# Two FFN norm rows by way of DRAM, and another order at the end of a convolution module, in a decoder trunk on one core

## The chip, the cores and the metric

The kernel runs on one core of one Trainium2 chip. The metric is the device time of one launch in microseconds. The engines are named as in the profile: PE is the matrix engine (PEld its weight loads), DVE the vector engine, ACT the scalar engine, POOL the GpSimd engine, SP the queue that issues most DMAs.

## The reference, cut to what matters

A trunk of four pre-norm residual sub-layers over 512 tokens and 1024 channels, in fp32: a retention and pooling mixer, an FFN, a convolution module, and a second FFN, with a final norm.

```python
def rms_norm(x, g):
    y = x * lax.rsqrt(jnp.mean(x * x, axis=-1, keepdims=True) + EPS)
    return y * g

def swiglu(h, w_gate, w_up, w_down):
    return (jax.nn.silu(h @ w_gate) * (h @ w_up)) @ w_down

def conformer_conv(h, w_pw1, b_pw1, w_dw, b_dw, ln_g, ln_b, w_pw2, b_pw2):
    a, gate = jnp.split(h @ w_pw1 + b_pw1, 2, axis=-1)
    u = a * jax.nn.sigmoid(gate)
    dw = causal_depthwise_conv(u, w_dw, width=31) + b_dw
    mu = jnp.mean(dw, axis=-1, keepdims=True)
    var = jnp.mean(jnp.square(dw - mu), axis=-1, keepdims=True)
    z = jax.nn.silu((dw - mu) * lax.rsqrt(var + EPS) * ln_g + ln_b)
    return z @ w_pw2 + b_pw2

x = x + swiglu(rms_norm(x, ffn_g), ...)      # after the mixer and after the conv module
x = x + conformer_conv(rms_norm(x, mix_g), ...)
```

## The kernel before

The activation X lies in SBUF with channels on partitions (eight tiles of 128) and the 512 tokens along the free side; the halves of 256 tokens are called A and B. Products run in fp32r, with each operand split into a high part and a rest: `mm3` issues high x high, high x rest and rest x high (lines 199 to 201). Splits are made while the kernel runs, ACT casting the high part and DVE or POOL's accumulating DMA making the rest; raw weight chunks of 1 MB arrive by SP's queue in two buffers (`wr`).

**Norm rows.** A norm needs one factor for each token, along the free side and equal on all partitions. `token_sums` multiplies `acc` (the squares summed over the channel tiles, 128 x 512) with a column of ones: four fp32 matmuls with 128 of the tokens each as weights, so that the sums come out with token 128t + p on partition p, column t of `ps_ms`. `inv_rms` makes the inverse root of them on DVE (`rs_y`, 128 x 4, three Newton steps, lines 264 to 271). `spread` turns it into a row on all partitions: four fp32 matmuls of `rs_y`'s broadcast columns with the unit matrix into `ps_rms` (line 289), and a copy by ACT into `bc_rms` (line 293). fp32 matmuls are two records each in the trace. In an FFN the factor is not applied to the input but to gate and up after their products (`hidden`, line 884, DVE). gu0 and gu1 are the first two column blocks of gate and up; `spread` stands between the products k = 4 and k = 5 of gu1, and `token_sums` at gu1's start.

**The conv module** is written in the order in which each engine is to run it. `proj(j)` is the first pointwise product of channel tile j (value and gate), `gated(j)` its sigmoid gate: DVE scales both by the norm's row, ACT takes the sigmoid (line 1192), DVE multiplies into `u` (line 1196). The channels' convolution runs in two ways. Tiles 0 to 2 are done on DVE, 31 taps each (`some_taps(n)`, line 1329, one multiply-add of 128 x 512 per tap). Tiles 3 to 7 are done on PE (`conv_tile`, line 1229): `to_rows` writes four shifted copies of `u` by DMA (tile `R`; for tile 5 the tile named `zh`, still unused then), and eight groups of four 32 x 32 diagonal products per quadrant add up the taps. `pivot_sum` and `pivot_mean` form a pivot from two tiles (token sums again, PE line 281, behind DVE's line 1301), which is spread as `mus` and taken from every tile before sums and squares are added up (`into_sums` for DVE's tiles, `pivot_tile` for PE's). `stats` makes mean and inverse deviation of a half (`ps_ms`, `ps_mu`, `ps_lrs`). `centre`, `swish`, `z_hi`, `z_lo` then make z, two tiles at a time, and split it (high `zh` by ACT, line 1288; rest `zl` by DVE). `out_proj(w, j, cols)` multiplies tiles j and j + 1 of z with four column blocks of the second pointwise weights into the PSUM pairs q0 and q1, for half A and then for half B; for each pair, `high_first` issues the eight products of the high part before the four with z's rest. `split_rest` splits a raw weight chunk in two parts with ACT and POOL's DMA (lines 1351, 1352); written as a generator, it is begun ahead of a `gated` and finished within it. PSUM holds three pairs of banks (`pmm`) and two single banks (`paux`).

Of the kernel before, what the change touches and what calls it, by code (L numbers as in the profile page):

```python
# [10 lines left out]
F32 = mybir.dt.float32  # L11
# [3 lines left out]
ALU = mybir.AluOpType  # L15
# [68 lines left out]
def trunk(ctx: ExitStack, tc: tile.TileContext, a: dict):  # L84
# [10 lines left out]
    paux = ctx.enter_context(tc.tile_pool(name="paux", bufs=2, space=PSUM))  # L95

# [115 lines left out]
    def high_first(ps, wh, wl, xh, xl, cols, ks, k0=0):  # L212

        for low in range(2):
            for k in ks:
                for i in range(2):
                    c = slice(i * P, (i + 1) * P)
                    o = ps[:, i, cols]
                    if low:
                        nc.tensor.matmul(o, lhsT=wh[:, k - k0, c], rhs=xl[k][:, cols], start=False, stop=k == KT - 1)  # L220
                    else:
                        nc.tensor.matmul(o, lhsT=wh[:, k - k0, c], rhs=xh[k][:, cols], start=k == 0, stop=False)
                        nc.tensor.matmul(o, lhsT=wl[:, k - k0, c], rhs=xh[k][:, cols], start=False, stop=False)

# [50 lines left out]
    def token_sums(acc, cols=FULL):  # L275

        ps = paux.tile([P, S], F32, tag="aux", name="ps_ms")
        n = (cols.stop - cols.start) // P
        for t in range(n):
            at = cols.start + t * P  # L280
            nc.tensor.matmul(ps[:, t:t + 1], lhsT=acc[:, at:at + P], rhs=ones, start=True, stop=True)
# [14 lines left out]
    def inv_rms(acc):  # L296
        v = sm.tile([P, NT], F32, tag="ms", name="ms")
        nc.vector.tensor_scalar(v, token_sums(acc), 0.5 / D, 0.5 * EPS, ALU.mult, ALU.add)
# [398 lines left out]
    def ffn_in(layer, acc, gain, fx, fl, fh, fe, ff):  # L697
# [278 lines left out]
        r = inv_rms(acc)  # L976
# [10 lines left out]
        feature_major(ps[1], *w, xgh, xgl, between={5: lambda: row.update(rb=spread(r, "rms"))})  # L987
# [178 lines left out]
    def conv(acc):  # L1166
        with ExitStack() as m:
# [54 lines left out]
            def conv_tile(j, cols, between={}, ps=None):  # L1222
                ps = ps if ps is not None else paux.tile([P, S], F32, tag="aux", name=f"ps_c{j}")
                n = cols.stop - cols.start
                for g in range(8):
# [137 lines left out]
            def out_proj(w, j, cols):  # L1363

                for i, q in enumerate((q0, q1)):
                    c = slice(2 * P * i, 2 * P * (i + 1))
                    high_first(q, w[0][:, :, c], w[1][:, :, c], zhs, zls, cols, range(j, j + 2), j // 4 * 4)
# [4 lines left out]
            with tc.manual_schedule(engines={mybir.EngineType.PE, mybir.EngineType.DVE, mybir.EngineType.Activation,  # L1372
# [43 lines left out]
                rest = split_rest()  # L1416
                next(rest)
                c3 = conv_tile(3, FULL)
                some_taps(1)
                gated(5, pss[5], FULL, two_taps, rest)  # L1420
                start_load()
                to_rows(5, FULL)
                bias_tile(3, c3)
                some_taps(14)
# [181 lines left out]
```

## Time and the profile before

| | us |
|---|---|
| median of 3 runs | 1047.19 (1046.95 to 1047.38) |
| the profiled execution | 1047.62 |
| its span, first to last instruction | 1045.8 |
| PE busy | 1035.9 (99%) |
| DVE busy | 850.5 (81%) |
| ACT busy | 515.9 (49%) |
| mean granted TensorE clock | 0.998 |

Rows of the profile read: start (or busy time), duration, engine, line, operation, output<-inputs, shape, and in brackets the idle time ahead of it with what ended it. xN joins N like instructions. A matmul's end is modelled and overlaps the next one's start, so PE is read by differences of starts. In lists of waits the numbers are the total in us, the count, and the longest. In lists of DMA issues the last number is the median time in us from issue to landing.

### The profile page before, as it was taken

Reading aid. Unit: us, or ns where it says so; the run is one execution under the profiler, and the core shown is the slowest. Engines: PE = TensorE matmul, PEld = TensorE weight load, DVE = VectorE, ACT = ScalarE, POOL = GpSimd, SP = SyncE. Lnnn points to the kernel's source line nnn. Section 1 sums busy time; section 2 is a strip of 40 time slices with the busy share of each in tenths; the row PEclk is TensorE's granted clock in tenths of the full one; section 3 lists DMA queues with packets and bytes.
Section 4 is the critical chain, followed back from the end, with each engine's and each line's share of the span. In section 5 each row is a group of like instructions: output and inputs, shape, how many; then the busy total and the mean of one; then the engine's idle time right before and its main releaser. Section 6 shows DMA issues by size and latency. Waiting matters only on the chain.

```text
span 1045.8 us, 16517 instructions
## 1 busy us (share of the span) xinstructions
PE 1035.9 (99%) x6705; PEld 907.9 (87%) x6705; DVE 850.5 (81%) x1297; ACT 515.9 (49%) x881; POOL 32.5 (3%) x33
## 2 busy tenths in 40 slices
PE   9999999999999999999999999999999999999997
PEld 7878888899999999998888665988999999999987
DVE  7888735889988889997779797859999888899855
ACT  8543134765454545543444325656654455445434
POOL 0000000100000000001121100000000000000000
PEclk9999999999999999999999999999999999999999
DMA  8322122643323322333248996146233332323122
GB/s 300 132 81 81 41 81 88 184 136 116 111 92 104 119 91 92 122 118 125 81 94 188 222 189 149 59 139 174 72 121 121 102 121 76 112 96 122 41 81 81
DMA packets 38108, 121.63 MB, mean 116 GB/s; under 512 B 4112, under 2 KB 13328, under 8 KB 29584
## 3 DMA queue, kind: packets, MB, share of 16 engines
q1 hardware_dynamic: 34432, 107.99, 32.4%
q0 software_dynamic: 3456, 12.58, 6.3%
q8 instruction: 52, 0.85, 0.3%
q14 instruction: 24, 0.20, 0.1%
q10 hardware_dynamic: 144, 0.00, 0.0%
HBM read 100.36 MB, written 2.10 MB: 98 GB/s over the span
## 4 chain that ended last, share of the span: by engine, by line
PE 88%; DVE 6%; ACT 2%; DMA 2%; issue 1%; DVEq 0%; ACTq 0%
PE ps_x L854 19%; PE ps_y L854 10%; PE ps_dn L199 7%; PE ps_dn L200 7%; PE ps_dn L201 7%; PE ps_z L854 5%; PE ps_c L1229 2%; PE ps_gu L201 2%; PE ps_gu L199 2%; PE ps_gu L200 2%; PE ps_pw L199 2%; PE ps_pw L201 2%; PE ps_pw L200 2%; DMA wr<-in_w_pw 2%; PE ps_wo L201 1%; PE ps_wo L200 1%
## 5 line engine op out<-in xcount | busy, mean ns | idle before, releaser
L854 PE MATMUL ps_x<-th,w 128*128 128x256 f32 x608 | 115.9, 276 | 0.3 <-ACT sn L929 0.3
L765 DVE TENSOR_TENSOR wg<-wg 128x512 f32<-128x512 f32 x152 | 105.3, 693 | 5.1
L774 ACT CAST w<-wg 128x512 fp32r<-128x512 f32 x152 | 82.9, 618 | 37.3 <-PE ps_y L854 36.0
L854 PEld LDWEIGHTS ps_x<-th,w 128*128 128x128 f32 x608 | 97.2, 188 | 0.5 <-ACT sn L929 0.5
L779 DVE TENSOR_TENSOR w<-wg,w 128x2048 fp32r<-128x2048 f32 x38 | 87.1, 2291 | 10.5 <-ACT w L774 10.1
L854 PE MATMUL ps_x<-tl,w 128*128 128x256 f32 x304 | 83.9, 276 | 0.0
L311 DVE TENSOR_TENSOR X<-X,ps_dn 128x1024 f32<-128x1024 f32 x46 | 56.0, 1218 | 18.6 <-PE ps_dn L201 18.6
L183 ACT CAST w<-wr 128x2048 fp32r<-128x2048 f32 (+2 forms) x22 | 34.8, 1599 | 56.6 <-PE ps_g L573 21.8
L199 PE MATMUL ps_dn<-hh,dh0d 128*128 128x512 f32 x152 | 59.4, 391 | 0.0
L200 PE MATMUL ps_dn<-hl,dh0d 128*128 128x512 f32 x152 | 59.4, 391 | 0.0
L201 PE MATMUL ps_dn<-hh,dl0d 128*128 128x512 f32 x152 | 59.2, 390 | 0.1
L854 PE MATMUL ps_y<-th,w 128*128 128x256 f32 x304 | 57.9, 276 | 0.0
L854 PE MATMUL ps_y<-xgh,w 128*128 128x256 f32 x304 | 57.9, 276 | 0.0
L854 PEld LDWEIGHTS ps_x<-tl,w 128*128 128x128 f32 x304 | 57.1, 188 | 0.0
L939 ACT COPY sn<-ps_x 128x256 f32<-128x256 f32 x38 | 14.2, 374 | 85.9 <-PE ps_x L854 85.9
L200 PE MATMUL ps_dn<-hl,dh1d 128*128 128x512 f32 x144 | 56.2, 391 | 0.0
L199 PE MATMUL ps_dn<-hh,dh1d 128*128 128x512 f32 x144 | 56.2, 391 | 0.0
L201 PE MATMUL ps_dn<-hh,dl1d 128*128 128x512 f32 x144 | 56.0, 389 | 0.0
L854 PE MATMUL ps_x<-xgh,w 128*128 128x256 f32 x288 | 55.2, 277 | 0.0
L878 DVE TENSOR_TENSOR hl<-act,hh 128x512 fp32r<-128x512 f32 x44 | 30.5, 692 | 26.3 <-ACT hh L877 26.1
L877 ACT CAST hh<-act 128x512 fp32r<-128x512 f32 x44 | 27.3, 621 | 48.0 <-DVE act L872 44.0
L199 PE MATMUL ps_pw<-xgh,w 128*128 128x512 f32 x128 | 50.3, 393 | 0.0
(346 smaller groups left out, 3098.9 us busy)
## 6 DMA issues: line engine op xcount, KB each, us to landing
wg<-in_w_gu SPq DMA_DIRECT2D x38, 1024.0 KB, 4.9
dr<-in_w_dn SPq DMA_DIRECT2D x64, 256.0 KB, 2.9
w<-wr POOLq DMA_DIRECT2D x24, 512.0 KB, 5.3
wr<-in_w_pw SPq DMA_DIRECT2D x10, 1024.0 KB, 5.1
wr<-in_w_gu SPq DMA_DIRECT2D x6, 1024.0 KB, 4.9
dr<-in_w_dn SPq DMA_DIRECT2D x32, 192.0 KB, 2.5
wr<-in_w_o SPq DMA_DIRECT2D x4, 1024.0 KB, 4.9
R<-u SPq DMA_DIRECT2D x12, 270.0 KB, 14.6
```

Of the source, the lines that this page charges most:

```text
L183: nc.scalar.copy(wh[:, s], raw[:, s])
L199: nc.tensor.matmul(out, lhsT=wh, rhs=xh, start=start, stop=False)
L200: nc.tensor.matmul(out, lhsT=wh, rhs=xl, start=False, stop=False)
L201: nc.tensor.matmul(out, lhsT=wl, rhs=xh, start=False, stop=stop)
L311: nc.vector.tensor_tensor(xx, xx, ps, sign)
L765: nc.vector.tensor_tensor(o, o, i, ALU.add)
L774: nc.scalar.copy(block(sums[f][0], *SUMS[i]), block(raw_g[f], *SUMS[i]))
L779: nc.vector.tensor_tensor(l, raw_g[f], h.bitcast(F32), ALU.subtract)
L854: nc.tensor.matmul(out, lhsT=u[:, k, :], rhs=v, start=first and k == 0 and n == 0, stop=k == 3 and n == 2, skip_group_check=True)
L877: nc.scalar.copy(hh[f], s)
L878: return lambda: nc.vector.tensor_tensor(hl[f], s, hh[f].bitcast(F32), ALU.subtract)
L1229: nc.tensor.matmul(ps[32 * i:32 * i + 32, :n], lhsT=dgs[j][:, i, g, :], rhs=Rs[j][:, i, 4 * g + cols.start:4 * g + cols.stop], start=g == ...
```

## The change

In both FFNs the norm's row goes by way of DRAM. `token_sums` gets `by=NT` (4): the weights of matmul t are tokens t, t + 4, t + 8 and so on (every fourth fp32 of `acc`), so that partition p holds tokens 4p to 4p + 3. `spread_row` writes `rs_y` to a row in DRAM with one DMA and reads it back with another, broadcast to all 128 partitions; both are issued by SP. `spread` and the ACT copy are gone there; the mixer's and the conv module's norms keep them.

At the end of the conv module:
- tiles 5, 6 and 7 are all done in halves, on PSUM pairs; tile 5's half B is cut in two by tile 7's half A;
- the last gate, gated(7), is done in halves, and it stands ahead of the sums of tiles 1, 4 and 5;
- two splits of weights (`split_rest`) stand behind the gates of tiles 5 and 6 instead of around them, and six more taps ahead of the pivot, two more in tile 4's stage, none at the end;
- the statistics of half A stand at the start of tile 6's half B, the spread of its inverse deviation ahead of tile 7's half B; the mean of half B is spread within an `out_proj`;
- `out_proj` issues all 16 products of z's high part for four column blocks, and then the eight of z's rest;
- in half B tiles 0 and 1 are multiplied, swished and cast one by one.

```diff
+    dr = ctx.enter_context(tc.tile_pool(name="dr", bufs=2, space=bass.MemoryType.DRAM))
...
-    def token_sums(acc, cols=FULL):
+    def token_sums(acc, cols=FULL, by=1):
 
         ps = paux.tile([P, S], F32, tag="aux", name="ps_ms")
         n = (cols.stop - cols.start) // P
+        if by > 1:
+            for t in range(n):
+                nc.tensor.matmul(ps[:, t:t + 1], lhsT=acc.rearrange("p (q t) -> p t q", t=n)[:, t, :], rhs=ones,
+                                 start=True, stop=True)
+            return ps[:, :n]
...
+    def spread_row(v, name):
+
+        row = dr.tile([S], F32, tag="row", name=f"row_{name}")
+        out = wk.tile([P, S], F32, tag=f"bc_{name}", name=f"bc_{name}", bufs=1)
+        nc.sync.dma_start(row.rearrange("(p t) -> p t", t=NT), v)
+        nc.sync.dma_start(out, row.partition_broadcast(P))
+        return out
+
+    def inv_rms(acc, by=1):
         v = sm.tile([P, NT], F32, tag="ms", name="ms")
-        nc.vector.tensor_scalar(v, token_sums(acc), 0.5 / D, 0.5 * EPS, ALU.mult, ALU.add)
+        nc.vector.tensor_scalar(v, token_sums(acc, by=by), 0.5 / D, 0.5 * EPS, ALU.mult, ALU.add)
         return rsqrt(v, NT, "a4")
...
-        r = inv_rms(acc)
+        row["rb"] = spread_row(inv_rms(acc, by=NT), "rms")
         load_gu(f0)
         plain_hi(f0)
...
-        feature_major(ps[1], *w, xgh, xgl, between={5: lambda: row.update(rb=spread(r, "rms"))})
+        feature_major(ps[1], *w, xgh, xgl)
...
-            def conv_tile(j, cols, between={}, ps=None):
+            def conv_tile(j, cols, between={}, ps=None, groups=range(8)):
...
-            def out_proj(w, j, cols):
-
-                for i, q in enumerate((q0, q1)):
-                    c = slice(2 * P * i, 2 * P * (i + 1))
-                    high_first(q, w[0][:, :, c], w[1][:, :, c], zhs, zls, cols, range(j, j + 2), j // 4 * 4)
+            def out_proj(w, j, cols, between=lambda: None):
+
+                (wh, wl), k0 = w, j // 4 * 4
+                for low in range(2):
+                    for i in range(4):
+                        if low == 0 and i == 2:
+                            between()
+                        o, c = (q0, q1)[i // 2][:, i % 2, cols], slice(i * P, (i + 1) * P)
+                        for k in (j, j + 1):
+                            if low:
+                                nc.tensor.matmul(o, lhsT=wh[:, k - k0, c], rhs=zls[k][:, cols], start=False,
+                                                 stop=k == KT - 1)
+                            else:
+                                nc.tensor.matmul(o, lhsT=wh[:, k - k0, c], rhs=zhs[k][:, cols], start=k == 0,
+                                                 stop=False)
+                                nc.tensor.matmul(o, lhsT=wl[:, k - k0, c], rhs=zhs[k][:, cols], start=False,
+                                                 stop=False)
...
                 some_taps(9)
-                rest = split_rest()
-                next(rest)
                 c3 = conv_tile(3, FULL)
                 some_taps(1)
-                gated(5, pss[5], FULL, two_taps, rest)
+                gated(5, pss[5], FULL, two_taps)
                 start_load()
                 to_rows(5, FULL)
+                for _ in split_rest():
+                    pass
                 bias_tile(3, c3)
-                some_taps(14)
+                some_taps(20)
                 proj(6)
-                rest = split_rest()
-                next(rest)
                 pivot_sum()
                 some_taps(1)
                 pivot_mean()
-                gated(6, pss[6], FULL, two_taps, rest)
+                gated(6, pss[6], FULL, two_taps)
                 to_rows(6, FULL)
-                c4 = conv_tile(4, FULL, {5: lambda: spread(row["piv"], "mu", piv)})
-                some_taps(4)
+                for _ in split_rest():
+                    pass
+                c4 = conv_tile(4, FULL, {4: lambda: spread(row["piv"], "mu", piv)})
+                some_taps(6)
                 nc.vector.scalar_tensor_tensor(s1, piv, -2.0, dsum, ALU.mult, ALU.add)
                 for i in PV:
                     into_sums(i, two_taps)
                 proj(7)
-                some_taps(8)
-                into_sums(2)
-                c5 = conv_tile(5, FULL)
-                gated(7, pss[7], FULL)
-                to_rows(7, A)
-                start_load()
-                to_rows(7, B)
+                into_sums(2, two_taps)
+                some_taps(NDVE * CW)
+                p5 = pair("ps_c5")
+                c5 = conv_tile(5, A, ps=p5[:, 0, :])
+                for cols in HALVES:
+                    gated(7, pss[7], cols)
+                    to_rows(7, cols)
+                    if cols is A:
+                        start_load()
                 nc.scalar.activation(warm, warm, AF.Silu)
-                some_taps(NDVE * CW)
-                into_sums(1)
-                pivot_tile(4, c4, FULL)
                 p6, p7 = [pair(f"ps_c{j}") for j in (6, 7)]
                 c6 = conv_tile(6, A, ps=p6[:, 0, :])
-                pivot_tile(5, c5, FULL)
+                pivot_tile(5, c5, A)
+                pivot_tile(4, c4, FULL)
+                into_sums(1)
+                c5 = conv_tile(5, B, ps=p5[:, 1, :], groups=range(4))
                 c7 = conv_tile(7, A, ps=p7[:, 0, :])
                 pivot_tile(6, c6, A)
                 pivot_tile(7, c7, A)
                 for _ in split_rest():
                     pass
-                c6 = conv_tile(6, B, ps=p6[:, 1, :], between={3: lambda: note("A", stats, A), 7: lambda: spread(row["A"][0], "mu", mus[:, A])})
+                conv_tile(5, B, ps=p5[:, 1, :], groups=range(4, 8))
+                c6 = conv_tile(6, B, ps=p6[:, 1, :], between={0: lambda: note("A", stats, A), 4: lambda: spread(row["A"][0], "mu", mus[:, A])})
+                c7 = conv_tile(7, B, ps=p7[:, 1, :], between={0: lambda: spread(row["A"][1], "lrs", lrs[:, A])})
                 centre(0, A)
-                c7 = conv_tile(7, B, ps=p7[:, 1, :], between={2: lambda: spread(row["A"][1], "lrs", lrs[:, A])})
+                pivot_tile(5, c5, B)
                 swish(0, A)
                 z_hi(0, A)
                 centre(2, A)
-                rest = pivot_tile(6, c6, B, True)
                 swish(2, A)
                 z_hi(2, A)
                 z_lo(0, A)
-                rest()
+                pivot_tile(6, c6, B)
                 centre(4, A)
                 swish(4, A)
                 z_hi(4, A)
                 z_lo(2, A)
-                rest = pivot_tile(7, c7, B, True)
+                later = pivot_tile(7, c7, B, True)
                 centre(6, A)
-                rest()
+                later()
                 swish(6, A)
                 z_hi(6, A)
...
-                out_proj(w1, 4, A)
-                spread(row["B"][0], "mu", mus[:, B])
+                out_proj(w1, 4, A, lambda: spread(row["B"][0], "mu", mus[:, B]))
                 spread(row["B"][1], "lrs", lrs[:, B])
                 z_lo(6, A)
                 out_proj(w1, 6, A)
                 centre(0, B)
-                swish(0, B)
-                z_hi(0, B)
+                for i in range(2):
+                    di = d[:, i, B]
+                    nc.vector.tensor_tensor(di, di, lrs[:, B], ALU.mult)
+                    nc.scalar.activation(di, di, AF.Silu, scale=V("ln_g", i), bias=V("ln_b", i))
+                    nc.scalar.copy(zh[:, i, B], di)
                 centre(2, B)
                 swish(2, B)
                 z_hi(2, B)
+                z_lo(0, B)
                 centre(4, B)
-                z_lo(0, B)
                 swish(4, B)
                 z_hi(4, B)
```

How this moves instructions is shown by the engines' order. PE in gu1 of the first FFN, ahead of and behind the spread (`xgh`, `xgl`: the two parts of the normed input's tile), before:

```order
L200 MATMUL ps_gu_1689<-xgl_1500,w_1553 128x512
L201 MATMUL ps_gu_1689<-xgh_1499,w_1553 128x512
L289 MATMUL ps_rms<-con,rs_y 128x128 x4
L199 MATMUL ps_gu_1689<-xgh_1506,w_1553 128x512
L200 MATMUL ps_gu_1689<-xgl_1507,w_1553 128x512
L201 MATMUL ps_gu_1689<-xgh_1506,w_1553 128x512
```

and after:

```order
L201 MATMUL ps_gu_1695<-xgl_1502,w_1555 128x512
L202 MATMUL ps_gu_1695<-xgh_1501,w_1555 128x512
L200 MATMUL ps_gu_1695<-xgh_1508,w_1555 128x512
L201 MATMUL ps_gu_1695<-xgl_1509,w_1555 128x512
L202 MATMUL ps_gu_1695<-xgh_1508,w_1555 128x512
```

The four fp32 products are gone from between the tiles. SP's queue in the same place (`dr`: down weights, `wg`: gate and up weights), before:

```order
L730 DMA dr_0_1560<-in_w_dn 128x384 x2
L730 DMA dr_1_1563<-in_w_dn 128x384 x2
L147 DMA wr_1670<-in_w_gu 128x2048
L720 DMA wg_4_1782<-in_w_gu 128x2048
L720 DMA wg_5_1833<-in_w_gu 128x2048
```

and after:

```order
L731 DMA dr_0_1562<-in_w_dn 128x384 x2
L731 DMA dr_1_1565<-in_w_dn 128x384 x2
L148 DMA wr_1676<-in_w_gu 128x2048
L293 DMA row_rms<-rs_y 128x4
L294 DMA bc_rms<-row_rms 128x512
L721 DMA wg_4_1781<-in_w_gu 128x2048
L721 DMA wg_5_1832<-in_w_gu 128x2048
```

The two DMAs of the row stand between a raw chunk and the next gate and up weights.

ACT in the conv module, from the sigmoid of gated(4) on (the second sigmoid is gated(5)'s; line 1242 is the bias of tile 3; CAST and ACTIVATE of `w` are the splits), before:

```order
L1192 ACTIVATE act<-gu,vec 128x512
L1351 CAST w_5444<-wr_5351 128x1024
L1352 ACTIVATE w_5444<-w_5444 128x1024
L1351 CAST w_5527<-wr_5433 128x1024
L1352 ACTIVATE w_5527<-w_5527 128x1024
L1192 ACTIVATE act<-gu,vec 128x512
L1351 CAST w_5527<-wr_5433 128x1024
L1352 ACTIVATE w_5527<-w_5527 128x1024
L1242 ACTIVATE d<-ps_c_5531,vec 128x512
L1351 CAST w_5648<-wr_5515 128x1024
L1352 ACTIVATE w_5648<-w_5648 128x1024
```

and after, from the end of the split that precedes gated(5):

```order
L1352 CAST w_5443<-wr_5350 128x1024
L1353 ACTIVATE w_5443<-w_5443 128x1024
L1193 ACTIVATE act<-gu,vec 128x512
L1352 CAST w_5576<-wr_5432 128x1024
L1353 ACTIVATE w_5576<-w_5576 128x1024
L1352 CAST w_5576<-wr_5432 128x1024
L1353 ACTIVATE w_5576<-w_5576 128x1024
L1243 ACTIVATE d<-ps_c_5526,vec 128x512
L1193 ACTIVATE act<-gu,vec 128x512
L1352 CAST w_5676<-wr_5514 128x1024
```

Two of the split's four operations stood ahead of gated(5)'s sigmoid; all four now stand behind it.

PE from the convolution of tile 5 to the first output product (`ps_c_5794`, then `ps_c_5793`: tile 5; `ps_c_5856` and `5850`: tile 6; `ps_c_5857` and `5851`: tile 7; 32 rows of the order are one half tile, and 64 records in the trace), before:

```order
L1229 MATMUL ps_c_5794<-zh,zf_5033 32x512 x32
L1229 MATMUL ps_c_5856<-R_5673,zf_5034 32x256 x32
L1229 MATMUL ps_c_5857<-R_5834,zf_5034 32x256 x32
L1229 MATMUL ps_c_5856<-R_5673,zf_5034 32x256 x12
L281 MATMUL ps_ms<-con,acc 128x1 x2
L281 MATMUL ps_ms<-con,s_5039 128x1 x2
L1229 MATMUL ps_c_5856<-R_5673,zf_5034 32x256 x16
L289 MATMUL ps_mu<-con,mean 128x128 x2
L1229 MATMUL ps_c_5856<-R_5673,zf_5034 32x256 x4
L1229 MATMUL ps_c_5857<-R_5834,zf_5034 32x256 x8
L289 MATMUL ps_lrs<-con,rs_y 128x128 x2
L1229 MATMUL ps_c_5857<-R_5834,zf_5034 32x256 x24
```

and after:

```order
L1230 MATMUL ps_c_5793<-zh,zf_5032 32x256 x32
L1230 MATMUL ps_c_5850<-R_5671,zf_5033 32x256 x32
L1230 MATMUL ps_c_5793<-zh,zf_5032 32x256 x16
L1230 MATMUL ps_c_5851<-R_5833,zf_5033 32x256 x32
L1230 MATMUL ps_c_5793<-zh,zf_5032 32x256 x16
L274 MATMUL ps_ms<-con,acc 128x1 x2
L274 MATMUL ps_ms<-con,s_5038 128x1 x2
L1230 MATMUL ps_c_5850<-R_5671,zf_5033 32x256 x16
L282 MATMUL ps_mu<-con,mean 128x128 x2
L1230 MATMUL ps_c_5850<-R_5671,zf_5033 32x256 x16
L282 MATMUL ps_lrs<-con,rs_y 128x128 x2
L1230 MATMUL ps_c_5851<-R_5833,zf_5033 32x256 x32
```

Tile 6's half A now follows half of tile 5, and half A's statistics stand ahead of tile 6's half B instead of within it.

More of the change, by code (lines that the diff above doesn't have):

```diff
@@ L210, in feature_major @@
                 mm3(ps[:, i, cols], wh[:, k, c], wl[:, k, c], xh[k][:, cols], xl[k][:, cols], k == 0, k == KT - 1)
[L212 to L223, printed above, removed]
     def split_scaled(h, l, src, scale):
@@ L294, in spread @@
         return out
-    def inv_rms(acc):
+    def spread_row(v, name):
[5 more added lines that the diff above has]
+    def inv_rms(acc, by=1):
         v = sm.tile([P, NT], F32, tag="ms", name="ms")
-        nc.vector.tensor_scalar(v, token_sums(acc), 0.5 / D, 0.5 * EPS, ALU.mult, ALU.add)
+        nc.vector.tensor_scalar(v, token_sums(acc, by=by), 0.5 / D, 0.5 * EPS, ALU.mult, ALU.add)
         return rsqrt(v, NT, "a4")
@@ L1220, in diagonals @@
                     C("mask32").unsqueeze(1).to_broadcast([P, 32, 32]), ALU.mult)
-            def conv_tile(j, cols, between={}, ps=None):
+            def conv_tile(j, cols, between={}, ps=None, groups=range(8)):
                 ps = ps if ps is not None else paux.tile([P, S], F32, tag="aux", name=f"ps_c{j}")
                 n = cols.stop - cols.start
-                for g in range(8):
+                for g in groups:
                     if g in between:
```

## The prediction

> **What bounds the kernel.** I read the page's busy times first, then the waits of PE, then the timelines at the places that the edits touch.
>
> ```profile
> PE 1035.9 (99%) x6705; PEld 907.9 (87%) x6705; DVE 850.5 (81%) x1297; ACT 515.9 (49%) x881; POOL 32.5 (3%) x33
> ```
> ```profile
> PE ps_idle L429 <- PEq L1595: 0.8, 1, 0.8
> PE ps_p L222 <- ACT zh L1288: 0.8, 2, 0.5
> PE ps_ms L281 <- DVE acc L1301: 0.3, 1, 0.3
> PE ps_x L854 <- ACT sn L929: 0.3, 1, 0.3
> PE ps_ms L281 <- DVE acc L256: 0.2, 1, 0.2
> ```
> PE is busy 1035.9 us of a span of 1045.8, and its waits (us in total, times, longest) are 2.4 us in all. So time is won in two ways only: instructions leave PE, or one of the last waits goes. What DVE or ACT save counts only where PE waits for them. The sum below is against the profiled execution's 1047.62 us, which is 0.43 above the median of the runs, 1047.19.
>
> **FFN: the spreads that leave PE.** In both FFNs the four fp32 products of `spread` (eight records) stand between the products of gu1.
>
> ```profile
> 200.47 0.39 PE L201 MATMUL ps_gu<-xgh,w 128*128 128x512 f32 x1
> 200.70 1.05 PE L289 MATMUL ps_rms<-con,rs_y 128*128 128x128 f32 x8
> 201.51 0.48 PE L199 MATMUL ps_gu<-xgh,w 128*128 128x512 f32 x1
> 201.82 0.39 PE L200 MATMUL ps_gu<-xgl,w 128*128 128x512 f32 x1
> ```
> I go by starts, since ends are modelled. A 512-wide product comes 0.23 us after the one before (200.47 to 200.70). The spread holds PE from 200.70 to 201.51, 0.81 us, and the product after it is 0.31 long instead of 0.23 (201.51 to 201.82), 0.08 more. That makes 0.9, and 1.8 us with the second FFN, which runs the same code. ACT's 512-wide copy out of PSUM goes too, worth nothing here, as no PE wait above names it.
>
> **FFN: the way by DRAM.** What takes the spread's place has to deliver `bc_rms` before DVE's first use of it.
>
> ```profile
> 197.99 0.16 DVE L271 SCALAR_TENSOR_TENSOR rs_y<-rs_t,rs_y 128x4 f32<-128x4 f32 x1
> ...
> 206.75 1.22 DVE L884 TENSOR_TENSOR gu<-ps_gu,bc_rms 128x1024 f32<-128x1024 f32 x1
> ...
> 219.63 1.83 DVE L759 TENSOR_TENSOR w<-wg,w 128x1024 fp32r<-128x1024 f32 x2 [1.51 <-ACT w L753]
> ```
> ```profile
> vg<-in_vec ACTq DMA_DIRECT2D x1, 4.0 KB, 3.1
> dr<-in_w_dn SPq DMA_DIRECT2D x64, 256.0 KB, 2.9
> w<-wr POOLq DMA_DIRECT2D x24, 512.0 KB, 5.3
> ```
> The scale is ready at 198.15 and first read at 206.75, 8.6 us later. The store of 2 KB is nearest to the 4 KB transfer, 3.1 us; the broadcast writes 256 KB, like `dr`, 2.9 us. As an estimate the row lands at 198.15 + 6.0 = 204.2. The bounds are 2.9 + 2.9 (204.0) and, if the load shares the engines with POOL's transfers of that stretch, 3.1 + 5.3 (206.6), still before 206.75. A little lateness has cover as well, as DVE idles 1.51 us soon after. So the way by DRAM costs nothing, hidden by 8.6 us of other DVE work; past about 10.1 us (8.6 and the 1.51) the multiply would hold the PSUM pairs of gu and PE would pay. Behind the two transfers on SP's queue stands the next weight load, which waits longer for its buffer anyway:
>
> ```profile
> SPq L720 <- DMA w<-wr: 15.1, 1, 15.1
> ```
>
> **FFN: the strided token sums.** To make the row contiguous in DRAM, `token_sums` now takes as weights every fourth fp32 of `acc`, 16 bytes apart. No row of before shows a load with such a stride.
>
> ```profile
> 192.95 0.95 PE L281 MATMUL ps_ms<-con,acc 128*128 128x1 f32 x8
> 193.76 0.49 PE L199 MATMUL ps_gu<-xgh,w 128*128 128x512 f32 x1
> ```
> ```profile
> L281 PEld LDWEIGHTS ps_ms<-con,acc x48: 186/192/192, 24.2 to 707.6; 128*128 128x128 f32 x48
> L1229 PEld LDWEIGHTS ps_c<-R,zf x256: 106/110/110, 632.2 to 648.7; 128*32 128x32 f32 x128
> ```
> The eight records take 0.81 us (192.95 to 193.76), 0.10 each, with one column of data: the weight load sets the pace. It is paid by the column: 128 columns last 192 ns, 32 last 110, so 0.85 ns for a column, 1.2 columns in a ns. Contiguous, four columns share 16 bytes; strided, each column is in another 16 bytes. The most that any row shows of that is the 512-wide moving operand, 2 KB in 0.23 us, 0.56 pieces of 16 bytes in a ns. If that is the limit, a strided load of 128 pieces takes 0.23 us instead of 0.10 to 0.11, 0.12 more, and the sixteen records of both FFNs 1.9 us. The lower bound is 0 (a read goes at 1.2 pieces in a ns as well as at 1.2 columns). A gain is excluded, for the same columns are loaded. [...] I take 1.9, the only one that rests on a rate seen here. With it the FFNs come out even: -1.8 + 1.9 = +0.1.
>
> [...]
>
> **The conv module.** Both halves of the edit move work past PE's waits there.
>
> ```profile
> 604.77 0.39 PE L201 MATMUL ps_pw<-xgh,w 128*128 128x512 f32 x1
> 605.45 1.05 PE L281 MATMUL ps_ms<-con,acc 128*128 128x1 f32 x8 [0.29 <-DVE acc L1301]
> ...
> 649.57 0.38 PE L222 MATMUL ps_p<-zh,w 128*128 128x256 f32 x1 [0.24 <-ACT zh L1288]
> ...
> 662.07 0.62 PE L220 MATMUL ps_p<-zl,w 128*128 128x256 f32 x4
> 663.22 0.38 PE L222 MATMUL ps_p<-zh,w 128*128 128x256 f32 x1 [0.53 <-ACT zh L1288]
> ```
> Pivot: the start of `ps_ms` comes 0.68 after the product ahead of it instead of 0.23, 0.45 lost to DVE's pivot sum. That sum is late because of this:
>
> ```profile
> 591.98 1.04 ACT L1351 CAST w<-wr 128x1024 fp32r<-128x1024 f32 x1 [10.97 <-DMA wr<-in_w_pw]
> 594.76 0.75 DVE L1196 SCALAR_TENSOR_TENSOR u<-gu,vec,act 128x512 f32<-128x512 f32 x1 [5.12 <-ACT act L1192]
> 595.43 0.75 DVE L1329 SCALAR_TENSOR_TENSOR d<-zf,vec,d 128x512 f32<-128x512 f32 x1
> ```
> ACT's split of a raw weight chunk waits for its DMA, the sigmoid of gated(5) stands behind it, and DVE idles 5.12 us. With the split moved behind gated(5), that idle time goes, and six more taps at 0.66 (594.76 to 595.43) fill 4.0 of it: the sum ends 1.1 earlier, and the 0.45 goes. The split is not late for its user: it is two pairs of operations of 1.05 each behind the sigmoid, over by 600, and proj(7) is 48 products of 0.23 that end where c5 starts, at 625.76 below, so it starts at 614.7.
>
> Half A: the first output product waited 0.24 for z. Statistics of A now stand before c6's half B instead of behind three of its eight groups (1.3 us earlier), so z is early and the 0.24 goes. Half B: 663.22 is 1.15 after the start of four 256-wide products, which take 0.45 (four halves of 0.23), so 0.70 lost. What it waits for is this pair of two-tile steps:
>
> ```profile
> 660.69 0.69 DVE L1283 TENSOR_TENSOR d<-d,lrs 128x512 f32<-128x512 f32 x1
> 662.54 0.62 ACT L1288 CAST zh<-d 128x512 fp32r<-128x512 f32 x1
> ```
> With tile 0's multiply, swish and cast apart from tile 1's, z of tile 0 comes about 0.6 earlier (half of 0.69 on DVE, half of 0.62 on ACT); I count 0.55. Putting rests last changes no count of products.
>
> What it may cost:
>
> ```profile
> 625.76 7.07 PE L1229 MATMUL ps_c<-zh,zf 128*32 128x512 f32 x64
> ```
> ```profile
> R<-u SPq DMA_DIRECT2D x2, 270.0 KB, 14.8
> L1229 PE MATMUL ps_c<-R,zf x256: 379/379/403, 632.7 to 649.0; 128*32 128x256 f32 x128
> ```
> c5 in two halves costs the same (7.07 us for 64 at full width; the four half tiles of 64 records each, c6 and c7, fill 632.7 to 649.3 with the statistics between, some 3.5 each without them). But c6's half A follows c5's half A, not all of c5: at 625.3 + 3.5 = 628.8 instead of 632.7. Its rows of u (`R`; the row is of the last two, issued at 614.5) land 14.8 later, 629.3, and the same transfers start perhaps 0.4 earlier now, with the pivot's wait gone ahead of them; I take 0.4 of new wait, between 0 and 1. More switches between conv groups and other products: 0.1, from the 0.08 of the spread. gated(7) in halves, the sums in another order and DVE's smaller operations lie where DVE idles for PE's tiles:
>
> ```profile
> 639.82 0.48 DVE L1257 SCALAR_TENSOR_TENSOR d<-ps_c,vec,mus 128x256 f32<-128x256 f32 x1 [2.00 <-PE ps_c L1229]
> ```
> They cost nothing as long as that 2.00 lasts. Conv: -0.45 - 0.24 - 0.55 + 0.4 + 0.1 = -0.7; bounds -1.4 (all waits gone, no new one) and +0.8 (below).
>
> **Sum.** +0.1 - 0.7 = -0.6, so 1047.0 beside the profiled 1047.62, and 1046.6 beside the median. 0.2% of it, 2.1 us, is about what a measurement of this kernel can tell from no change.
>
> **The rivals.**
> - Strided loads are free. [...] Then -1.8 - 0.7 = -2.5, 1044.7: faster.
> - New waits in conv's end. c6's half A waits 1 us for its rows, and the first product of q1, which takes over the PSUM pair of c6 (its half B is read by DVE behind a rest of z now, where it stood ahead of it), waits 0.5. That product comes 8 products of 0.11 after half A's start at 648.9 (649.57 - 0.45 - 0.24), at 649.8, and DVE's read falls within some tenths of that. Then -0.45 - 0.24 + 1.5 = +0.8 in conv, with half-pace loads +0.9: 1048.1, within 0.2%.
> [...]
> - The row lands late: beyond 10.1 us after the scale, each us costs PE one us in each FFN. The longest bound above is 8.4, so I give it little; at 12 us the sum is -0.6 + 2 x 1.9 = +3.2, 1050.4.
>
> **Chances.** Half-pace loads with conv's gain 0.42, free loads 0.29, new waits 0.14, quarter pace 0.10, late row 0.05. The forecast is the first, 1046.6, its own range 1045.6 to 1047.6. The range holds the first three: the free loads with all conv waits gone are 1047.19 - 3.2 = 1044.0, so 1044.0 to 1048.3; what is left out is 0.15 and some tails. Faster by over 0.2% is most of the free loads (0.24; the rest of it is just short of 2.1) and 0.06 of the first case, 0.30. Slower is the last two, 0.14 of their 0.15. Same is the rest, 0.56.
>
> **What would show it.** No `ps_rms` records inside gu1, and the products there at 0.23 throughout. The eight `ps_ms` records of the FFN: 0.81 us if strides are free, 1.7 at half pace, 3.4 at a quarter. L884's successor in DVE's order starts without a wait for `bc_rms`. In PE's waits no row for the pivot's `ps_ms`; perhaps one for c6's rows; the one before half B down to 0.15. I am wrong if PE waits for DVE's first scaled gu, if a wait at q1's first product appears, or if the sums' pace is neither of the three.

## The result and the profile after

The changed kernel is slower by two parts in a thousand: 1049.9 us median of 12 runs (1047.15 to 1052.72) against 1047.95 of 12 runs of before (1046.95 to 1049.69), ratio 1.0021, 95% interval 1.0013 to 1.003. Its profiled execution took 1048.85 us with a span of 1047.1, 1.2 us more than that of before, so it is one of its quicker executions. In some executions of the kernels here, before among them, the granted clock is 0.994 to 0.997 instead of 0.998 or 0.999 and the time mostly longer (before's eight such, at 0.996 or 0.997, took 1050.46 to 1053.28, its others at most 1050.6); the three longest of the changed kernel (1052.0 to 1052.72, clock 0.996) are such, as are four of eleven of c5_whole and of old_out and five of six of plain_sums below, but the median of the changed kernel's other nine is 1049.63, so its loss stands without them.

PE's waits in the changed kernel (total in us, times, longest):

```profile
PE ps_c L1230 <- DVE d L1258: 0.8, 1, 0.8
PE ps_idle L430 <- PEq L1613: 0.8, 1, 0.8
PE ps_gu L202 <- DMA w<-wr: 0.4, 1, 0.4
PE ps_x L855 <- ACT sn L930: 0.3, 1, 0.3
PE ps_ms L274 <- DVE acc L244: 0.2, 1, 0.2
PE ps_qk L200 <- ACT w L355: 0.2, 1, 0.2
```
The pivot's wait and the two waits for z are gone, as forecast. New are 0.8 us at a conv tile (`ps_c`) and 0.4 at the weights of gu (`w<-wr`).

The strided sums, by form, beside those that stayed contiguous (min, median and max of one in ns), and the eight products of the first FFN:

```profile
L274 PEld LDWEIGHTS ps_ms<-con,acc x32: 186/192/192, 24.7 to 656.7; 128*128 128x128 f32 x32
L269 PEld LDWEIGHTS ps_ms<-con,acc x16: 308/329/332, 193.2 to 709.3; 128*128 128x128 f32 x16
```
```profile
193.44 1.80 PE L269 MATMUL ps_ms<-con,acc 128*128 128x1 f32 x8
```
A strided load of 128 columns lasts 329 ns instead of 192, 0.137 us more. Nothing but the stride differs. The loads overlap (eight of them take 1.94 us on PEld, not 8 times 0.329), so what they cost PE is read by starts: from the first of the eight products to the product behind them it is 1.66 us (193.44 to 195.10, and 707.96 to 709.62 in the second FFN), where it was 0.81. That is 0.85 more in each FFN and 1.7 in both, 0.12 for each further product. The expectations below reckon with 16 times 0.137, 2.2 us, which is too much.

The way by DRAM, from the lists of DMA issues around the first FFN's row (KB, us to landing):

```profile
bc_rms<-row_rms SPq DMA_DIRECT2D x1, 256.0 KB, 4.2
row_rms<-rs_y SPq DMA_DIRECT2D x1, 2.0 KB, 1.4
```
5.6 us in all, inside the 8.6 of cover; PE has no wait that goes back to `bc_rms`.

The conv module on PE, from the pivot to the end of the output products:

```profile
605.46 0.39 PE L202 MATMUL ps_pw<-xgh,w 128*128 128x512 f32 x1
605.68 0.95 PE L274 MATMUL ps_ms<-con,acc 128*128 128x1 f32 x8
...
625.90 3.66 PE L1230 MATMUL ps_c<-zh,zf 128*32 128x256 f32 x64
630.35 3.66 PE L1230 MATMUL ps_c<-R,zf 128*32 128x256 f32 x64 [0.79 <-DVE d L1258]
633.80 1.94 PE L1230 MATMUL ps_c<-zh,zf 128*32 128x256 f32 x32
635.52 3.66 PE L1230 MATMUL ps_c<-R,zf 128*32 128x256 f32 x64
...
651.46 0.28 PE L1379 MATMUL ps_p<-zh,w 128*128 128x256 f32 x1
651.71 0.38 PE L1377 MATMUL ps_p<-zh,w 128*128 128x256 f32 x1
651.93 0.28 PE L1379 MATMUL ps_p<-zh,w 128*128 128x256 f32 x1
...
664.15 0.28 PE L1379 MATMUL ps_p<-zh,w 128*128 128x256 f32 x1
664.42 0.39 PE L1377 MATMUL ps_p<-zh,w 128*128 128x256 f32 x1
664.65 0.28 PE L1379 MATMUL ps_p<-zh,w 128*128 128x256 f32 x1
```
A half tile without a wait lasts 3.46 from start to start (635.52 less 633.80 is 1.72 for half of one), so tile 6's half A should start at 629.36 and starts at 630.35, 1.0 late. q1's first product (651.71) comes 0.25 after the one ahead of it, and the next 0.22 later, where 0.11 is the pace: 0.25 lost. DVE reads the PSUM pair that it takes over until 651.66 (line 1258, 0.48 from 651.18). Half B's second z (664.42) loses 0.27 in the same way, where the wait of before cost 0.70.

### The profile page after: what moved, and what is told of

Read it like the earlier page. It is cut to its first block, busy times and chain, and to the rows that moved or that the text cites. A ratio compares the mean times of both kernels' runs of the same rounds, so it can differ in the third digit from the quotient of the medians.

```text
span 1047.1 us, 16622 instructions
## 1 busy us (share of the span) xinstructions
PE 1037.1 (99%) x6753; PEld 912.2 (87%) x6753; DVE 851.0 (81%) x1303; ACT 515.4 (49%) x882; POOL 32.5 (3%) x33
## 4 chain that ended last, share of the span: by engine, by line
PE 87%; DVE 6%; ACT 4%; DMA 2%; issue 1%; DVEq 0%; ACTq 0%
PE ps_x L855 19%; PE ps_y L855 10%; PE ps_dn L200 7%; PE ps_dn L201 7%; PE ps_dn L202 7%; PE ps_z L855 5%; PE ps_c L1230 3%; PE ps_pw L200 3%; PE ps_pw L202 2%; PE ps_pw L201 2%; PE ps_wo L202 1%; PE ps_wo L201 1%; PE ps_wo L200 1%; PE ps_qk L200 1%; PE ps_qk L201 1%; PE ps_qk L202 1%
```

## The experiments

All ratios are to the kernel before, run beside them on the same chip, with 95% intervals.

**1. Which part is it?** ffn_only has the FFN edits alone, conv_only the conv module's alone.

> The kernel before with the FFN part of the change alone (strided token sums, row by way of DRAM, no spread); the conv module as before. Theory 1 (the FFN part comes out even, the loss is in the conv module): the strided weight load lasts 329 ns where the contiguous one lasts 192, 0.14 us more for each of 16 records, 2.2 us, against 1.8 us of spreads, so +0.0 to +0.5 us against before. Theory 2 (the way by DRAM disturbs other transfers of the FFN, and PE waits for a weight chunk): about +2 us, with PE waits of 0.4 us and more for w<-wr in the FFNs. Theory 3 (neither part: the runs of the changed kernel merely drew a lower clock): within 0.3 us of before, in this run and in the other three.

> The kernel before with the conv module's end of the change alone; both FFNs with spread and contiguous token sums. Theory 1: the pivot's 0.45 us goes, tile 6's half A waits 1.0 us or more for its rows of u, the output products give back what half B's wait had cost: +0.8 to +2 us against before. Theory 2: -0.5 to +0.3 us. Theory 3: 0.

ffn_only: 1048.03 us, ratio 1.0002 (0.9993 to 1.001). conv_only: 1050.23 us, 1.0018 (1.0002 to 1.0034), and with times from 1047.06 to 1053.18, no wider than those of before beside it (1047.12 to 1053.28). By the medians the loss is the conv module's, though the two intervals overlap. The longest waits of PE, ffn_only first, then conv_only:

```profile
PE ps_gu L202 <- DMA w<-wr: 1.0, 1, 1.0
```
```profile
PE ps_c L1216 <- issue: 1.8, 1, 1.8
```
The FFN part has the new wait for `w<-wr` by itself, 1.0 here, in the second FFN. The conv part has the wait at the conv tile, 1.8 here and 1.0 in the changed kernel; the profile names another releaser each time.

**2. What does tile 6 wait for?** c5_first puts half of tile 5's half B ahead of tile 6's half A; c5_whole puts all of it there and leaves out the other half's later place.

```diff
+                c5b = conv_tile(5, B, ps=p5[:, 1, :], groups=range(4))   # c5_whole: all groups
                 c6 = conv_tile(6, A, ps=p6[:, 0, :])
...
-                c5 = conv_tile(5, B, ps=p5[:, 1, :], groups=range(4))
+                c5 = c5b
```

> The changed kernel with the first half of tile 5's half B (four of eight groups, 1.7 us) ahead of tile 6's half A instead of behind it. Theory 1 (tile 6's half A waits for its rows of u, which land 15 us after they are issued): the 1.0 us of wait goes, 1.0 us faster than the changed kernel. Rival (it waits for DVE's pivot step of tile 5's half A, as the profile names it): the wait stays, within 0.2 us of the changed kernel or slower, as DVE's step comes no earlier.

> The changed kernel with both halves of tile 5 ahead of tile 6's half A, so that this half starts some 3.5 us later, where it started before the change; all else as changed. Theory 1 (what made the changed kernel slow is the wait of tile 6's half A for its rows of u, which land between 629 and 633 from run to run): no PE wait there, and 2 us faster than the changed kernel, 0 to -1 us against before. Rival (half A's wait only moves on, to the statistics or the output products, which start at the same time as before): within 0.5 us of the changed kernel, +1.5 to +2.5 against before.

c5_first: 1047.86 us, 1.0002 (0.9993 to 1.001), below the changed kernel's interval. Its profile, of an execution of 1049.62, the second longest of its eleven, names the cause:

```profile
PE ps_c L1230 <- DMA R<-u: 2.0, 1, 2.0
```
It is the rows of u. In this execution they were so late that even a start 1.7 us later waited 2.0. The four transfers took 18.1 us in the median here, 15.6 in the changed kernel's profile (c5_first's list of issues, then the changed kernel's):

```profile
R<-u SPq DMA_DIRECT2D x4, 270.0 KB, 18.1
```
```profile
R<-u SPq DMA_DIRECT2D x4, 270.0 KB, 15.6
```
Taken one by one, the last of tile 6's four rows lands just ahead of PE's start in all three profiles with the wait, whatever releaser the profile names:

| | last row issued | us to landing | landed | tile 6 starts on PE |
|---|---|---|---|---|
| before | 614.50 | 14.6 | 629.1 | 632.66, no wait |
| changed kernel | 614.53 | 15.6 | 630.1 | 630.35 |
| conv_only | 615.94 | 15.7 | 631.6 | 631.80 |
| c5_first | 614.83 | 18.1 | 632.9 | 633.16 |

c5_whole had no wait at the tile, but came to 1048.6 us, 1.0009 (1.0 to 1.0017), not the 0 to -1 us expected. The half tile moved was the cover of half A's statistics:

```profile
PE ps_ms L274 <- ACT sqc L1247: 1.2, 1, 1.2
```
So the rival was right in part: a wait moved on to the statistics. c5_whole_conv is the same conv module with the FFNs of before.

> The same order of tile 5 and 6, with the conv module's part of the change alone (spread and contiguous token sums in both FFNs). Theory 1: pivot -0.45, half B -0.55, output products +0.4, so -0.3 to -0.8 us against before, and no wait for w<-wr in the FFNs. Rival (the FFN part is what gains): +0.5 us or more against before.

1048.98 us, 1.0006 (0.9996 to 1.0015), between the two expectations: the same wait of 1.2, none in the FFNs. That the two can't be told apart says again that the FFN part is about even.

**3. The statistics back at their old place.** c5_late is c5_whole with half A's statistics behind three groups of tile 6's half B, and DVE's pivot step of that tile ahead of z's rest.

```diff
-                c6 = conv_tile(6, B, ..., between={0: lambda: note("A", stats, A), 4: ...})
+                c6 = conv_tile(6, B, ..., between={3: lambda: note("A", stats, A), 7: ...})
...
-                z_lo(0, A)
                 pivot_tile(6, c6, B)
+                z_lo(0, A)
```

> The changed kernel with tile 5 whole ahead of tile 6's half A, half A's statistics again behind three groups of tile 6's half B (mean spread ahead of group 7, deviation ahead of group 2 of tile 7), and DVE's pivot step of tile 6's half B ahead of z's rest of tiles 0 and 1. Theory 1: no wait for rows, none for the statistics (1.2 us in c5_whole), none at q1's first product (0.24 us with its restart): the conv module 0.8 to 1.2 us shorter than before, the FFNs +0.1 to +0.9, so -1 to +0.2 us against before. Rival: half A's z comes too late again and PE waits there, +0.5 or more.

1049.24 us, 1.0012 (1.0003 to 1.0021): the expectation fell, its rival held.

```profile
PE ps_p L1377 <- ACT zh L1289: 0.9, 1, 0.9
PE ps_p L1374 <- DVE zl L1296: 0.9, 1, 0.9
```
Half A's z is late. Yet from tile 6's start to the first output product it is 17.6 us (632.46 to 650.02), against 17.9 in c5_whole (632.05 to 649.94) with its 1.2 of wait at the early statistics: with tile 5 whole ahead of tile 6, the early place gains nothing there. What c5_late loses on top is the wait for the rest, and that belongs to the other move: ahead of the rest (652.31) DVE now does the pivot step, in which it idles 1.59 for ACT's `sqc`.

**4. The rows earlier.** load_later is the changed kernel with one line moved: the raw chunk of 1 MB that SP issued ahead of the rows of tiles 5 and 6 goes behind them.

```diff
                 gated(5, pss[5], FULL, two_taps)
-                start_load()
                 to_rows(5, FULL)
...
                 to_rows(6, FULL)
+                start_load()
```

> The changed kernel with one edit: the raw weight chunk of 1 MB that SP issues right after gated(5), ahead of the rows of tiles 5 and 6, is issued after the rows of tile 6 (its split stands at half B of tile 6, some 30 us later). Theory 1 (tile 6's half A waits for rows that stand in line behind other transfers): 1 MB less ahead of them, some 2.5 us at the 400 GB/s that a chunk alone reaches, so that the rows land near 627 instead of 630, no PE wait at tile 6's half A, 1 to 2 us faster than the changed kernel. Rival (the rows are slow by themselves, pieces of 128 rows with four taps each): they still take 15 us, and the wait stays.

The 400 GB/s are those of a chunk of 1 MB in before's first FFN: 5.0 us from issue to landing, and 351 to 421 GB/s in the slices from 195.9 to 198.0.

1047.5 us, 0.9993 (0.9983 to 1.0003), with times from 1046.77 to 1049.32. The interval lies wholly below the changed kernel's: the place of this one line is what made the changed kernel slower. In the list of issues and on PE:

```profile
R<-u SPq DMA_DIRECT2D x4, 270.0 KB, 7.8
```
```profile
626.08 3.66 PE L1230 MATMUL ps_c<-zh,zf 128*32 128x256 f32 x64
629.55 3.64 PE L1230 MATMUL ps_c<-R,zf 128*32 128x256 f32 x64
```
The rows take 7.8 us in the median instead of 15.6, and tile 6 starts 3.47 after tile 5, with no wait. The four are far apart, 4.4 to 13.7, and the last is the one that counts: it is issued at 612.25 instead of 614.53 and takes 13.7 instead of 15.6, so it lands at 626.0 instead of 630.1. More than half of these 4.1 us come from the earlier issue.

**5. The order of the output products.** old_out is c5_whole with the order of before.

```diff
-            def out_proj(w, j, cols, between=lambda: None):
-                ...
+            def out_proj(w, j, cols):
+                for i, q in enumerate((q0, q1)):
+                    c = slice(2 * P * i, 2 * P * (i + 1))
+                    high_first(q, w[0][:, :, c], w[1][:, :, c], zhs, zls, cols, range(j, j + 2), j // 4 * 4)
```

> The kernel c5_whole with the output products in the order of before (for each PSUM pair eight products of z's high part, then four with its rest; half B's mean spread between two calls). Theory 1 (the new order costs some 0.5 us over the stretch of half A: one more change of weights around the spread, and q1's first product earlier than its PSUM pair is free): the stretch from the first output product to the first 512-wide one is 0.3 to 0.6 us shorter than in c5_whole. Rival (the order is free): the same length within 0.1 us; or longer, if the rests z_lo come too late in the old order.

1050.23 us, 1.0018 (1.0009 to 1.0027). From the first output product to the first 512-wide one it took 25.2 us (651.78 to 676.96) against 24.8 in c5_whole (649.94 to 674.71), so the new order is better by 0.4 here, against theory 1. The rival's second case held, the old order meets late rests:

```profile
PE ps_p L221 <- DVE zl L1309: 0.5, 1, 0.5
```
Before, with z's rests in their old places, the stretch took 24.7 (649.57 to 674.25), in the changed kernel 24.8 (650.52 to 675.29).

**6. The stride by itself.** stride_only is the kernel before with strided sums; the spread stays, and ACT's copy puts the row in order.

```diff
-        r = inv_rms(acc)
+        r = inv_rms(acc, by=NT)
...
-        nc.scalar.copy(out, ps[:, :n * P])
+        nc.scalar.copy(out.rearrange("p (q t) -> p t q", t=by), ps[:, :n * P].rearrange("p (t q) -> p t q", t=by))
```

> The kernel before with strided token sums in both FFNs, and the spread kept (ACT's copy puts the row in order). Half pace, as in the changed kernel's trace (329 for 192 ns of load, 0.24 for 0.10 us of pace): +2.2 us against before, and the eight records take 1.9 us from start to start. If the strided load is paid only where a DMA writes beside it, the pace here stays under 0.2 and the time within 1 us of before.

The load is 329 ns again, and the eight products take 1.66 us, but the time is 1048.85 us, 1.0011 (1.0002 to 1.0019): about 1.1 us, between 0.2 and 2.0, and not the 1.7 that PE lost. Its list of PE's waits has no row for the pivot's 0.3 us of before: PE comes later to a place where it waited, and waits less. That gives back the 0.45 lost at the pivot; another 0.36 comes back at gu2 (experiment 7), where its products now follow each other at 0.23 throughout. What is left of 1.7 is 0.9, and the spans of the two profiled executions differ by 0.8 (1046.6 and 1045.8). So not all of PE's time ahead of the conv module sets the end.

**7. The spread by itself.** plain_sums is the changed kernel with contiguous sums and a scattered store; perm_ffn is the kernel before with contiguous sums, the fast store and a reordering copy by ACT.

```diff
-        nc.sync.dma_start(row.rearrange("(p t) -> p t", t=NT), v)
+        nc.sync.dma_start(row.rearrange("(t p) -> p t", p=P), v)              # plain_sums
...
+            nc.scalar.copy(out.rearrange("p (t q) -> p t q", t=NT), raw.rearrange("p (q t) -> p t q", t=NT))   # perm_ffn
```

> The changed kernel with contiguous token sums again; the row is put in order by the store to DRAM instead, 512 pieces of 4 bytes in place of 128 of 16. Theory 1: the sixteen records of the sums fall back from 0.24 to 0.10 us, 2.2 us faster than the changed kernel, so about even with before, if the scattered store still lands within the 8.6 us of cover. Theory 2: no faster than the changed kernel, or slower, as more small transfers disturb more. If the store takes over 6 us, PE waits for DVE's first scaled gu instead.

> The kernel before with the row by way of DRAM in both FFNs, but contiguous token sums and the fast store of 16-byte pieces; the row arrives in another order of tokens (4p + t for 128t + p) and ACT's copy, where the spread's copy stood, puts it in order by a strided read. Theory 1 (the strided weight load cancels the spread's 1.8 us): -1.8 us against before, less 0 to 1 us of PE wait for the weight chunk whose accumulating DMA runs beside the row's transfers. Theory 2 (PE's time in the FFN does not set the end, since a DMA does right after): within 0.5 us of before, and a wait for w<-wr that is longer by what PE gained.

plain_sums: 1055.57 us, 1.0074 (1.0057 to 1.0091). The store of 512 pieces of 4 bytes takes 9.1 us, and POOL's accumulating DMA beside it 7.9 where it takes 5.0 in the changed kernel and 4.6 in before:

```profile
row_rms<-rs_y SPq DMA_DIRECT2D x1, 2.0 KB, 9.1
```
```profile
w<-wr POOLq DMA_DIRECT2D x1, 512.0 KB, 7.9
```
```profile
PE ps_gu L202 <- DMA w<-wr: 5.5, 2, 3.9
```
DVE waits 4.67 for the late row, but PE's waits are for the weights' rest. perm_ffn: 1048.26 us, 1.0001 (0.9991 to 1.0011). No stride, no spread, fast transfers, and no gain; theory 2 held. Its waits, and its PE at gu2 with that of before:

```profile
PE ps_gu L202 <- DMA w<-wr: 2.5, 2, 1.7
```
```profile
206.12 0.50 PE L202 MATMUL ps_gu<-xgh,w 128*128 128x512 f32 x1 [0.79 <-DMA w<-wr]
```
```profile
206.16 0.49 PE L201 MATMUL ps_gu<-xgh,w 128*128 128x512 f32 x1
206.49 0.40 PE L199 MATMUL ps_gu<-xgh,w 128*128 128x512 f32 x1
```
The third product of gu2 needs the weights' rest. In before it stood at 206.16 with no wait worth a row, only a longer step to its successor (0.33 for 0.23); with the spread gone PE comes there 1.0 earlier (the product ahead starts at 204.94 instead of 205.93) and still starts at 206.12. In before that rest comes by this transfer, issued at 201.5:

```profile
w<-wr POOLq DMA_DIRECT2D x1, 512.0 KB, 4.6
```
It lands at 206.1, and the chain of raw chunk, ACT's split and this accumulating DMA sets the time at which gu2 can go on. In the second FFN perm_ffn waits 1.71 at the same product and starts it at 720.43. Before was late there already, 0.15 at this product and 0.11 at its successor:

```profile
719.91 0.39 PE L200 MATMUL ps_gu<-xgl,w 128*128 128x512 f32 x1
720.29 0.50 PE L201 MATMUL ps_gu<-xgh,w 128*128 128x512 f32 x1
720.63 0.40 PE L199 MATMUL ps_gu<-xgh,w 128*128 128x512 f32 x1
```
The spread had been free.

**8. The chain given cover.** gu2_last is perm_ffn with gu2's products in another order; final adds load_later's conv module; strided_final is final with the changed kernel's strided sums. both (perm_ffn, c5_late and load_later together) was run ahead of these.

```diff
-        feature_major(ps[2], *w, xgh, xgl)
+        for low in range(2):          # all products of the weights' high part, then those of their rest
+            for k in range(KT):
+                ...
```

> perm_ffn's FFNs, c5_late's conv module and load_later's order of the raw chunk together. Theory 1: the sum, -2 to -3 us against before, faster than both kernels. Theory 2: -0.5 to -1, the conv module's part alone.

> perm_ffn (the kernel before, spread out of both FFNs, contiguous sums) with the products of the third gate-and-up block, gu2, in another order: all that use the high part of the weights first, those with the weights' rest last, some 7 us later. In perm_ffn PE waited 0.8 and 1.7 us at gu2 for that rest, which a chain of transfer, split and accumulating DMA delivers at a time of its own. Theory A (the spread's 1.8 us were hidden behind this chain, and become a gain once the chain has cover): no wait for w<-wr at gu2, 1.5 to 2.5 us faster than before. Theory B (another wait takes its place, DVE's scaled gu or the next blocks of weights): within 0.5 us of before, with that wait in PE's list.

> gu2_last's FFNs with load_later's conv module. Theory A: -1.8 from the FFNs and about -0.5 from the conv module, 2 to 3 us faster than before, and than the changed kernel by 4 or more. Theory B: within 0.5 us of load_later.

> The same with the changed kernel's strided token sums in place of ACT's reordering copy (load_later with gu2's products in the new order). If PE's time ahead of gu2 counts now, the strided weight loads cost 16 x 0.137 = 2.2 us more than final. If it doesn't, the two are equal within 0.5 us.

both: 1049.16 us, 1.0007 (0.9998 to 1.0015), no gain, with c5_late's two waits and 2.2 us for `w<-wr`. gu2_last: 1045.08 us, 0.9976 (0.9967 to 0.9984). final: 1044.95 us, 0.9972 (0.9961 to 0.9983). strided_final: 1046.45 us, 0.9991 (0.9982 to 0.9999). Theory A held: with the chain covered, the spreads' 1.8 us and a little more come out. final is faster than before by 2.9 us and than the changed kernel by more. Its waits of PE:

```profile
PE ps_idle L455 <- PEq L1638: 0.8, 1, 0.8
PE ps_ms L294 <- DVE acc L269: 0.2, 1, 0.2
PE ps_x L880 <- ACT sn L955: 0.2, 1, 0.2
```
Between strided_final and final lie 0.0019 of the ratio, 2.0 us (1.5 by the medians), and every execution of final is shorter than every one of strided_final: now the stride counts in full (1.7). gu2's order alone, with the spread kept, was not tried; what before lost at gu2 is 0.10 in the first FFN and 0.26 in the second, so by its trace there is 0.4 us to win. What the conv module adds in final (0.4 us by the ratios) is within the intervals.

## Why the prediction was wrong, point by point

The step that failed is the term for tile 6's rows: the forecast put 0.4 us of wait there, and load_later, which takes that wait away, lies 2.9 us below the changed kernel. With 2.9 in place of 0.4 the forecast's sum of -0.6 comes to +1.9, where +2.2 was measured. A second step, PE as the bound, failed as well, but in this kernel the strided loads hid it.

- **PE as the bound: wrong for the FFNs.** "Instructions leave PE, or one of the last waits goes" took PE's 2.4 us of waits to mean that all its other time counts. At gu2 it had under 0.1 us of margin (landing at 206.1, use at 206.16): the forecast did not ask how long before their use the weights landed. The spreads left, 0.9 each, as worked out, and perm_ffn gave all of it back 5 us later.
- **Strided sums: right.** 0.12 more was forecast for each product and 0.12 measured, 1.7 us in all for 1.9 forecast; the load itself became 0.137 longer, 329 ns for 192. The eight records take 1.66 us, so the 0.81 of free strides is out, and no run shows the 3.4 of a quarter of the pace. Nor is it shown what in the load is slower: 16 bytes is the only stride that was run, and that the load is paid by the piece of 16 bytes was an estimate from the pace of the moving operand.
- **The FFNs even: right in the sum, by luck in part.** On PE it is -1.8 and +1.7, and ffn_only's 1.0002 fits the +0.1. But the two terms do not count by themselves: alone, the spreads' removal gains nothing (perm_ffn), and the stride costs about 1.1 (stride_only, between 0.2 and 2.0).
- **The way by DRAM: right in its own time**, 5.6 us (6.0 was forecast). Missed was the second FFN's wait for the weights' rest, 0.4 in the changed kernel and 1.0 in ffn_only, at the same place without margin; that the row's transfers slow the accumulating DMA is shown only for the scattered store of plain_sums (7.9 us for 4.6 in before).
- **Pivot: right.** `ps_ms` starts 0.22 after the product ahead of it, no wait. But the 0.45 was one execution's: with the conv module of before, this wait is 0.8 in ffn_only's profile, 0.9 in gu2_last's and none in perm_ffn's. Half A's first product has none either, and half B's 0.70 has become 0.27.
- **Tile 6's rows: the term that was mis-sized, and the one that decides.** Forecast 0.4, between 0 and 1; measured 1.0 and 1.8 in two profiles, and 2.0 at a start 1.7 later in a third. The forecast took one execution's landing time, 629, for a constant and set the issue 0.4 earlier; in the changed kernel the last row was issued as before (614.53 for 614.50), and in the three profiles it landed at 630.1, 631.6 and 632.9. It was the end of a queue behind a 1 MB chunk that ACT did not read until 640.15; before, tile 6 came more than 3 us after the landing and didn't see it vary.
- **Output products.** The rival's wait at q1 came, 0.25 instead of 0.5, and for the reason that it gave, DVE's late read of tile 6's half B. Together with half B's 0.27 and 0.08 behind the mean's spread, which now stands by itself (the first product after it, at 658.76, takes 0.20 to its successor instead of 0.12), that is 0.60 of the 0.70 that half B had waited; the stretch is no shorter, 24.8 us for 24.7.
- **The sum.** The rival "new waits in conv's end" was the one that happened, at 1048.1 by the forecast. Measured against before's median in the same runs it is +2.2, where the forecast's range ended at +1.1. The rest is the size of the rows' wait, for which load_later against the changed kernel gives 2.9 us (1.0021 less 0.9993; 1.0 to 4.9 by the ends of the two intervals). Not all of it need be this wait: the changed kernel's profiled execution, one of its quicker ones, shows 1.0, and the chunk's later transfer may help elsewhere. That the sum with it comes so near is luck in part, for the forecast also left out the FFNs' wait of 0.4.

Open is which transfer makes the rows later in one execution than in the next; and the 0.5 us that the profiled execution of the changed kernel lost in the program's first 7 us, where nothing was changed.

## What to carry to other kernels

A short list of waits does not make an engine's time count (perm_ffn took 1.8 us off PE, for a ratio of 1.0001): ask of each of its inputs how long before use it landed, and expect a gain ahead of a landing without margin to come back as a wait there. Where a step is moved ahead of other work, the landing time of its data is to be taken with its spread (here 629.1 to 632.9 in four profiles), and with what stands ahead of it in the queue; a large transfer that is not needed soon may be able to go behind, as in load_later, where the last row landed at 626.0. Products that use the part of the operands that is made last belong at the end of their group: that one reordering turned a change without effect into 2.5 us.

## What the runs showed of the hardware

A weight load of 128 fp32 columns 16 bytes apart takes 329 ns, contiguous 192; products of one column behind such loads start 0.23 us apart instead of 0.11. A store of 2 KB to DRAM takes 1.4 to 1.6 us in 128 pieces of 16 bytes, and 9.1 in 512 pieces of 4; beside the latter an accumulating DMA of 512 KB took 7.9 us, beside the former 5.0, and 4.6 in before without either. Four transfers of 270 KB landed after 4.4 to 13.7 us when 1 MB less stood ahead of them, and after 13.2 to 18.4 otherwise.
